# One layer-order change in a two-layer encoder: operands of a pair one step earlier, other orders at the first and last blocks, a third value tile

## The chip, the cores and the metric

The kernel runs on one core of one Trainium2 chip. The metric is the device time of one launch in microseconds (us); the kernel before took 4037.84 us in the median of three runs (4030.55 to 4040.72). The core has five engines with a queue each: TensorE (PE, matrix products into the PSUM banks), VectorE (DVE), ScalarE (ACT), GpSimd (POOL) and SyncE (SP), which here only issues transfers. Each engine works through its own list of instructions in order, and waits at an instruction until what it needs is there.

## The reference, cut to what matters

Two layers work on 256 prompt tokens and 1024 sample tokens, with 1024 channels, in float32. Layer 0 mixes tokens with a bidirectional RWKV recurrence, layer 1 with a two-dimensional neighbourhood attention; each is followed by the same kind of channel mixer, and that is where most of this change lies:

```python
def _sq_relu_mlp(h, w_up, w_down):
    return jnp.square(jax.nn.relu(h @ w_up)) @ w_down

for layer in range(DEPTH):
    h = _rms_norm(x, p['norm_mix_g'][layer])
    y = mixer(h)                    # RWKV in layer 0, attention in layer 1
    x = x + y
    x = x + _sq_relu_mlp(_rms_norm(x, p['norm_mlp_g'][layer]), p['w_up'][layer], p['w_down'][layer])
```

The hidden width is 4096. Both products of the mixer are 1280 tokens by 1024 by 4096.

## The kernel before, in words

A float32 product is made from three matmuls of rounded halves. Each operand is cut into a high half (a cast on ACT) and a low half (operand minus high half, on DVE or POOL); the products high·high, high·low and low·high are summed in PSUM. So every operand costs a cast and a subtraction before PE can use it. In the names, `ah`/`al` are the halves of the normed activations, `whi`/`wlo` those of `w_up` (L90, L91), `dh`/`dl` those of `w_down` or of sums of its tiles, and `hh`/`hl` those of the hidden values (L1371, L1372; True marks a sample half, False the prompt).

The tokens are worked in three segments: 0 is the prompt (256 columns), 1 and 2 are the halves of the sample (512 columns each). The hidden width is worked in 32 blocks `f` of 128. `up(f, s)` makes block `f` for segment `s`: 24 matmuls, a relu on ACT (L1387), a square on POOL (L1388), and, where it is wanted at once, the cut into halves. The cut of a prompt block is made within `up` in every case. `wup(f)` loads and cuts the next `w_up` tile, its low half on POOL. `wraw(f, i)` only issues the load of half `i` of a `w_down` tile on SP, from a ring of six buffers, and `wdown` loads and cuts. `down` (L1420 adds the product to the residual `x`) is the plain second product of one or two blocks for one segment; the last one also scales `x`, writes it out (L1423) and, in layer 0, prepares the attention's normed activations.

Blocks 2 to 29 are worked in pairs by a scheme with seven products in place of eight for the sample halves. `prep(n)` forms the two operands of product `n`, as sums (L1435) where needed, and cuts both: the weights' side in `wcut` (ACT, POOL) and the values' side in `bcut` (ACT, DVE). `product(n)` issues 12 matmuls (L1480 to L1482) into four banks of kind `pc`, and adds each to a part of `x` on DVE (L1484), four adds. A product that starts a new group of sums needs its four banks empty, so it waits for the adds of the product before it that used them. `prompt(n)` multiplies the same weights with the prompt's block (24 matmuls of 256 columns) and has two adds (L1495) on DVE.

`block_pair` gives the order by hand: while the products of one pair run, it interleaves the `up` steps of the next two blocks `f2` and `f3 = f2 + 1`. `prep(0)` of the next pair (`ahead[0](0)`) is the last operand made in this order, behind `prompt(7)`. In the last pair there is no next pair (`final`), and three `up` steps of blocks 30 and 31 are left. PE, DVE, ACT and POOL follow this written order closely; SP's order and all of the attention's orders are made by a scheduler that places work by its own estimates of times.

At a layer's end the last two blocks go through plain downs in the order of the segments. In layer 0 the norms of each segment's tokens (`N(s)`, with a small matmul at L1196) and the first quarter of the attention's values (`V(tb)`, one of ten blocks of 128 tokens: 24 matmuls at L513 to L515, a scaled copy `vt` on ACT at L519, a write at L520) follow inside them. The other three quarters of the values come afterwards, with `vt` in a ring of two.

Of the kernel before, what the change touches and what calls it, by code (L numbers as in the profile page):

```python
# [5 lines left out]
F32 = mybir.dt.float32  # L6
# [7 lines left out]
P = 128  # L14
# [37 lines left out]
class Trunk:  # L52
# [1222 lines left out]
    def channel_layer(self, layer, x_src, src, wname, dst, gnext=None, gate=False):  # L1275
# [3 lines left out]
        nc, tc, a, act = self.nc, self.tc, self.a, self.act  # L1279
        NF = 32  # L1280
        gmlp = V_GMLP + 8 * layer
        with ExitStack() as ctx:
# [42 lines left out]
            def wup(f):  # L1325
                wu[f] = self.wsplit(wp, a["w_up"][layer, f], 1024, nc.gpsimd, tag="u", rb=1)
# [28 lines left out]
            def scale(s):  # L1355
                c0, c1 = SEGS[s]
                n = c1 - c0
                ps = pn.tile([P, 512], F32, name="nps", tag="nps")
                nc.tensor.matmul(ps[:, :n], ones, ms[s], start=True, stop=True)
                nc.vector.tensor_scalar(out=ms[s], in0=ps[:, :n], scalar1=1.0 / (KT * P), scalar2=RMS_EPS, op0=ALU.mult, op1=ALU.add)  # L1360
                for m in range(8):
                    (nc.gpsimd if m % 2 else nc.vector).tensor_tensor(out=x[s][:, m], in0=x[s][:, m], in1=ms[s], op=ALU.mult)
# [5 lines left out]
            def split(src, s, pool, tags, bufs, eng):  # L1368
                n = src.shape[1]
                hi, lo = (pool.tile([P, n], F32R, name=t, tag=t, bufs=bufs) for t in tags)  # L1370
                nc.scalar.copy(hi, src)  # L1371
                eng.tensor_tensor(out=lo, in0=src, in1=hi.bitcast(F32), op=ALU.subtract)  # L1372
                return hi, lo

            def cut(f, s, last=False):
                r = hid[f, s]
                if last:
                    hid[f, s] = split(r, s, wh_, ("tt", "tt"), 2, nc.vector)
                else:
                    hid[f, s] = split(r, s, wh_, (f"hh{s > 0}", f"hl{s > 0}"), 3 if s else 4, nc.vector)  # L1380

            def up(f, s, name=None, whole=True):
                c0, c1 = SEGS[s]
                n = c1 - c0
                ps = dense(*wu[f], s, name)
                r = wk.tile([P, n], F32, name="rl", tag="nt", bufs=6) if s else wh_.tile([P, n], F32, name="rl", tag="np", bufs=2)
                nc.scalar.activation(r, ps[:, :n], AF.Relu)  # L1387
                nc.gpsimd.tensor_tensor(out=r, in0=r, in1=r, op=ALU.mult)  # L1388
                hid[f, s] = r
                if whole or s == 0:  # L1390
                    cut(f, s)
# [106 lines left out]
            def block_pair(f2, cur, ahead):  # L1498

                (prep, product, prompt), f3, final = cur, f2 + 1, ahead is None  # L1500
                U = lambda f, s: up(f, s, "ps", False)
                prep(1)
                product(0)
                U(f2, 1)
                wraw(f3, 0)
                prompt(0)
                prep(2)
                product(1)
                U(f2, 2)
                wraw(f2, 1)  # L1510
                prep(3)
                product(2)
                U(f2, 0)
                if not final:
                    wup(f2 + 2)
                prep(4)
                product(3)
                U(f3, 1)
                wraw(f3, 1)
                prompt(3)  # L1520
                prep(5)
                product(4)
                prep(7)
                if not final:
                    U(f3, 2)
                prep(6)
                product(5)
                U(f3, 0)
                wraw(f2, 0)
                if not final:  # L1530
                    wup(f3 + 2)
                prompt(7)
                if not final:
                    ahead[0](0)
                product(6)
                prompt(6)

# [3 lines left out]
            vw = []  # L1541
# [3 lines left out]
            N = lambda s: lambda: norms(s)  # L1545
            V = lambda tb: lambda: block(tb)
            up(0, 0)
            wup(1)
            scale(0)
            wdown(0)  # L1550
            up(1, 0)
            up(0, 1)
            up(1, 1)
            scale(1)
            up(0, 2)
# [8 lines left out]
            with tc.manual_schedule(engines=MANUAL):  # L1564
# [17 lines left out]
                for f in range(2, NF - 2, 2):  # L1582
                    ahead = pair_steps(f + 2, f + 3) if f < NF - 4 else None
# [4 lines left out]
            with tc.manual_schedule(engines={mybir.EngineType.PE}):  # L1588
                wdown(NF - 2, False)
                cut(NF - 2, 1)  # L1590
                wdown(NF - 1, False)
                cut(NF - 1, 1)
                cut(NF - 2, 2)
                up(NF - 1, 2, None, False)
                cut(NF - 1, 2, True)
                down([NF - 2, NF - 1], 0)
                if gnext is None:
                    down([NF - 2, NF - 1], 1)
                    down([NF - 2, NF - 1], 2)
                else:  # L1600

                    v0 = [self.wsplit(wp, a["w_nv"][0, :, 4 * j:4 * j + 4, :].rearrange("p k c -> p (k c)"), 1024, nc.gpsimd, tag="u", rb=1) for j in range(2)]
                    vw += [tuple(t[:, 256 * (k % 4):256 * (k % 4) + 256] for t in v0[k // 4]) for k in range(KT)]
                    down([NF - 2, NF - 1], 1, {6: [N(0)]})
                    down([NF - 2, NF - 1], 2, {1: [V(0)], 3: [V(1)], 4: [N(1)], 5: [V(2)]})
                    for f in (V(3), V(4), N(2), V(5), *map(V, range(6, 10))):
                        f()


# [24 lines left out]
    def attention(self):  # L1634
        nc, tc, a, act = self.nc, self.tc, self.a, self.act
        v1_d = self.scr["v1_d"]
        vs_d = self.dram("vs_d", [20, P, 1024])
        at_d = self.dram("at_d", [8, 2, P, T])
        with ExitStack() as ctx:
            pool = lambda name, c=ctx, bufs=1, **kw: c.enter_context(tc.tile_pool(name=name, bufs=bufs, reuse_waits="tile", **kw))  # L1640
            self.awp = pool("atw", bufs=2, side="right")
            self.apd = pool("apd", bufs=2, space=PSUM)
            self.gq = self.awp.tile([P, 1], F32, name="gq", bufs=1)
            nc.vector.tensor_scalar(out=self.gq, in0=self.vec[:, V_QG:V_QG + 1], scalar1=0.125, scalar2=None, op0=ALU.mult)
            self.awp.tile([P, 20], F32, name="rs", tag="rs", bufs=4)
            J, work, tail = self.qk_proj(0)

            self.qke = [pool("qk0"), None]
            self.qlo = [self.low_queries(self.qke[0]), None]
            bp = pool("abp")  # L1650

            self.bs = [bp.tile([P, 2, 3, 12, 32], F32, name=f"bs{r}") for r in range(2)]
            self.bpm = bp.tile([P, 2, 2, 128], F32, name="bpm")
            for t in self.bs:
                nc.vector.memset(t, NEG)
            with ExitStack() as c2:
                vp = pool("atv", c2)
                pv = pool("apv", c2, 3, space=PSUM)


                vp.tile([P, 256], F32, name="vt", tag="vt", bufs=2)
                vw = [None, self.v_weights(a["w_nv"], vp, 1)]
                work.pop(1)()
                bias = self.load_bias(0, 0, []) + self.load_bias(0, 1, []) + self.load_bias(0, 2, [])
                for q in range(1, 4):
                    if q < 3:
                        vw.append(self.v_weights(a["w_nv"], vp, q + 1))
                    for tb in range(10):
                        self.v_block(act, vw[q], v1_d, (vp, "vt", 256, 2), (pv, "vps"), q, tb, self.tn[:, 0, tb:tb + 1])
                        if tb == 3:  # L1670
                            self.strips(q - 1, nc.scalar)
                        for f in bias[:2]:
                            f()
                        del bias[:2]
            self.qk = self.qke[1] = pool("aqk", bufs=2)
            self.qlo[1] = self.low_queries(self.qk)
            self.awk = pool("awk", bufs=2)
            self.apn = pool("apn", space=PSUM)
            self.aps = pool("aps", bufs=2, space=PSUM)
            self.apt = pool("apt", bufs=2, space=PSUM)  # L1680
            self.apo = pool("apo", space=PSUM)
            self.attend_all(J, work, tail)
# [410 lines left out]
```

## Time and profile before

| what | us |
|---|---|
| median of three runs | 4037.84 (4030.55, 4037.84, 4040.72) |
| profiled execution, its time | 4028.49 |
| its span | 4026.7 |
| PE busy | 3754.7 |
| DVE busy | 2394.2 |
| ACT busy | 1686.2 |
| POOL busy | 1697.3 |
| mean granted clock of PE | 0.969 |

The mixer of layer 0 begins at about 1500 us and its blocks end at 2360; the attention's values and its other products follow up to about 3042; the mixer of layer 1 runs from about 3130 to the end. A row of a timeline gives start, duration, engine, line, operation, output and inputs, shape, count, and in brackets how long the engine stood idle before it and what ended that. A matmul's duration overlaps with the next one's; PE's pace is read from the distance of two starts. A row of a window gives the stretch, its length, the busy time and count of PE, PEld (weight loads), DVE, ACT and POOL, then the granted clock of PE (1.00 is full), the busy share of the transfer engines, and GB/s.

### The profile page before, as it was taken

The page shows a single profiled execution, that of the slowest core. Times are in us where ns is not written, and L with a number is a line of the kernel's source. Part 1 is how long each engine was busy: PE and PEld are TensorE (multiplying, and loading weights), DVE is VectorE, ACT ScalarE, POOL GpSimd, SP SyncE. Part 2 cuts the span into 40 slices and gives each one's busy share as a digit, 9 for nine tenths or more (in the row PEclk, how much of TensorE's full clock was granted, in tenths as well). Part 3 has the DMA queues.
Part 4 walks back from the last instruction along what each step waited for, and adds up shares of the span by engine and source line. Part 5 has one row for each costly group of instructions (what it writes and reads, how often), then busy time and mean ns, then how long its engine had stood idle before and what let it go on. Part 6 is the DMA issues. An engine that isn't in the chain of part 4 may idle for free.

```text
span 4026.7 us, 89828 instructions
## 1 busy us (share of the span) xinstructions
PE 3754.7 (93%) x36484; PEld 3158.2 (78%) x36484; DVE 2394.2 (59%) x4441; ACT 1686.2 (42%) x4128; POOL 1697.3 (42%) x1540
## 2 busy tenths in 40 slices
PE   8988888889888899999999988999989999999999
PEld 5764578778888787888888878887778788888887
DVE  5778743656464445666666671355553656666666
ACT  6777642555555431222222242466663222222221
POOL 4446641122222424545555561344442455555454
PEclk9988999999999899999999999999999999999999
DMA  4236565776664430111111115345465111111111
GB/s 138 73 98 226 211 222 136 163 172 159 160 148 122 130 104 27 42 37 40 38 37 42 40 61 159 114 108 112 98 157 169 37 40 37 43 40 43 37 40 61
DMA packets 460094, 394.83 MB, mean 98 GB/s; under 512 B 268480, under 2 KB 353856, under 8 KB 459680
## 3 DMA queue, kind: packets, MB, share of 16 engines
q1 hardware_dynamic: 425264, 327.73, 29.5%
q10 hardware_dynamic: 34416, 61.35, 4.2%
q8 instruction: 288, 4.72, 0.5%
q14 instruction: 126, 1.03, 0.1%
HBM read 270.50 MB, written 124.44 MB: 98 GB/s over the span
## 4 chain that ended last, share of the span: by engine, by line
PE 67%; DVE 8%; ACT 7%; issue 6%; DMA 5%; POOL 5%; SPq 1%; ACTq 0%; POOLq 0%; DVEq 0%
PE ps L96 12%; PE ps L97 11%; PE ps L98 11%; PE wu L998 4%; PE ps L1480 4%; PE ps L1482 3%; PE ps L1481 3%; POOL rl L1388 1%; PE vps L513 1%; ACT whi L90 1%; PE aps L998 1%; POOL dl L1372 1%; PE vps L514 1%; PE vps L515 1%; PE op L2005 1%
## 5 line engine op out<-in xcount | busy, mean ns | idle before, releaser
L96 PE MATMUL ps<-ah,whi 128*128 128x512 f32 (+1 forms) x2304 | 845.1, 367 | 4.7 <-ACT whi L90 3.9
L98 PE MATMUL ps<-ah,wlo 128*128 128x512 f32 (+1 forms) x2304 | 826.2, 359 | 9.5 <-POOL wlo L91 9.3
L97 PE MATMUL ps<-al,whi 128*128 128x512 f32 (+1 forms) x2304 | 827.6, 359 | 0.0
L98 PEld LDWEIGHTS ps<-ah,wlo 128*128 128x128 f32 x2304 | 435.3, 189 | 84.0 <-POOL wlo L91 10.5
L96 PEld LDWEIGHTS ps<-ah,whi 128*128 128x128 f32 x2304 | 436.6, 189 | 79.9 <-issue 9.0
L97 PEld LDWEIGHTS ps<-al,whi 128*128 128x128 f32 x2304 | 436.8, 190 | 65.7 <-issue 1.0
L1484 DVE TENSOR_TENSOR x<-ps,x 128x512 f32<-128x512 f32 x784 | 484.9, 678 | 0.0
L1388 POOL TENSOR_TENSOR rl<-rl 128x512 f32<-128x512 f32 (+1 forms) x192 | 173.8, 905 | 658.7 <-ACT rl L1387 381.6
L1387 ACT ACTIVATE rl<-ps 128x512 f32<-128x512 f32 (+1 forms) x192 | 101.0, 526 | 799.2 <-PE ps L98 799.2
L91 POOL TENSOR_TENSOR wlo<-raw,whi 128x1024 fp32r<-128x1024 f32 (+1 forms) x114 | 235.2, 2063 | 228.0 <-ACT whi L90 220.5
L1480 PE MATMUL ps<-hhTrue,dh 128*128 128x512 f32 x784 | 309.6, 395 | 21.8 <-DVE x L1484 21.8
L1482 PE MATMUL ps<-hhTrue,dl 128*128 128x512 f32 x784 | 308.0, 393 | 0.5 <-POOL dl L1372 0.5
L1481 PE MATMUL ps<-hlTrue,dh 128*128 128x512 f32 x784 | 308.0, 393 | 0.0
L1372 DVE TENSOR_TENSOR hlTrue<-rl,hhTrue 128x512 fp32r<-128x512 f32 x98 | 122.1, 1247 | 202.6 <-ACT hhTrue L1371 202.3
L1372 POOL TENSOR_TENSOR dl<-raw,dh 128x512 fp32r<-128x512 f32 x128 | 221.0, 1729 | 11.0 <-ACT dh L1371 7.0
L1372 DVE TENSOR_TENSOR hlTrue<-ts,hhTrue 128x512 fp32r<-128x512 f32 x112 | 131.2, 1171 | 150.3 <-ACT hhTrue L1371 150.3
L90 ACT CAST whi<-raw 128x1024 fp32r<-128x1024 f32 (+1 forms) x142 | 133.2, 938 | 190.0 <-PE ps L97 81.6
L1371 ACT CAST dh<-ds 128x512 fp32r<-128x512 f32 x112 | 69.5, 620 | 295.5 <-POOL ds L1435 295.5
L1480 PEld LDWEIGHTS ps<-hhTrue,dh 128*128 128x128 f32 x784 | 147.8, 188 | 53.9 <-issue 27.1
L1495 DVE TENSOR_TENSOR x<-ps,x 128x512 f32<-128x512 f32 x224 | 148.7, 685 | 68.0 <-PE ps L98 66.7
L1372 POOL TENSOR_TENSOR dl<-ds,dh 128x512 fp32r<-128x512 f32 x112 | 157.3, 1405 | 63.5 <-ACT dh L1371 63.5
L1942 POOL TENSOR_TENSOR s<-s,mx 128x384 f32<-128x384 f32 (+1 forms) x150 | 109.7, 744 | 163.0 <-DVE mx L1941 115.7
(339 smaller groups left out, 10268.1 us busy)
## 6 DMA issues: line engine op xcount, KB each, us to landing
raw<-in_w_down_dram SPq DMA_DIRECT2D x128, 256.0 KB, 2.7
raw<-in_w_up_dram SPq DMA_DIRECT2D x64, 512.0 KB, 3.4
ar<-ar_d SPq DMA_DIRECT2D x80, 256.0 KB, 4.2
bk<-bk_d SPq DMA_DIRECT2D x80, 256.0 KB, 3.6
ar_d<-ar ACTq DMA_DIRECT2D x32, 512.0 KB, 3.1
bk_d<-bk ACTq DMA_DIRECT2D x32, 512.0 KB, 4.7
bs<-tab SPq DMA_DIRECT2D x128, 96.0 KB, 3.8
v_d<-vt ACTq DMA_DIRECT2D x80, 128.0 KB, 3.3
```

The costliest lines, as they stand in the source:

```text
L90: nc.scalar.copy(hi[:, cs], raw)
L91: lo_eng.tensor_tensor(out=lo[:, cs], in0=raw, in1=hi[:, cs].bitcast(F32), op=ALU.subtract)
L96: mm(ps, sh, mh, start=first, stop=False)
L97: mm(ps, sh, ml, start=False, stop=False)
L98: mm(ps, sl, mh, start=False, stop=last)
L998: self.nc.tensor.matmul(out, w, x, start=start, stop=stop, skip_group_check=free)
L1372: eng.tensor_tensor(out=lo, in0=src, in1=hi.bitcast(F32), op=ALU.subtract)
L1388: nc.gpsimd.tensor_tensor(out=r, in0=r, in1=r, op=ALU.mult)
L1480: mm(ch[j], hi[:, cs], hh, start=bool(new), stop=False, skip_group_check=True)
L1481: mm(ch[j], hi[:, cs], hl, start=False, stop=False, skip_group_check=True)
L1482: mm(ch[j], lo[:, cs], hh, start=False, stop=True, skip_group_check=True)
L1484: nc.vector.tensor_tensor(out=xv, in0=ch[j], in1=xv, op=ALU.add)
```

## The change

There are four edits to the order of steps, and one buffer more.

- In `block_pair`, for all pairs but the last, `prep(0)` of the next pair moves from behind `prompt(7)` to ahead of `U(f3, 0)`, and `wraw(f2, 0)` is issued ahead of it too. PE's own order is the same in these pairs.
- In the last pair `U(f3, 0)` moves from behind `product(5)` to ahead of `prep(6)`.
- At the first blocks `up(0, 1)` moves up, from behind `up(1, 0)` to right behind `wup(1)`.
- At the last blocks the down of segment 0 moves ahead of `up(31, 2)`; in layer 0 the value blocks and norms are put in another order: `V(0)` stands ahead of the down of segment 2, `V(1)` inside it, and `N(1)` behind it.
- In the attention `vt` gets three buffers in place of two.

```diff
                 prep(7)
-                if not final:
-                    U(f3, 2)
+                U(f3, 0 if final else 2)
                 prep(6)
                 product(5)
-                U(f3, 0)
                 wraw(f2, 0)
                 if not final:
+                    ahead[0](0)
+                    U(f3, 0)
                     wup(f3 + 2)
                 prompt(7)
-                if not final:
-                    ahead[0](0)
                 product(6)
                 prompt(6)
...
             up(0, 0)
             wup(1)
+            up(0, 1)
             scale(0)
             wdown(0)
             up(1, 0)
-            up(0, 1)
             up(1, 1)
...
+                down([NF - 2, NF - 1], 0)
                 up(NF - 1, 2, None, False)
                 cut(NF - 1, 2, True)
-                down([NF - 2, NF - 1], 0)
...
                     down([NF - 2, NF - 1], 1, {6: [N(0)]})
-                    down([NF - 2, NF - 1], 2, {1: [V(0)], 3: [V(1)], 4: [N(1)], 5: [V(2)]})
-                    for f in (V(3), V(4), N(2), V(5), *map(V, range(6, 10))):
+                    V(0)()
+                    down([NF - 2, NF - 1], 2, {1: [V(1)]})
+                    for f in (N(1), *map(V, range(2, 6)), N(2), *map(V, range(6, 10))):
                         f()
...
-                vp.tile([P, 256], F32, name="vt", tag="vt", bufs=2)
+                vp.tile([P, 256], F32, name="vt", tag="vt", bufs=3)
```

How DVE's list changes at one passage from a pair to the next, in layer 0. Before (`hlTrue<-ts` is the low half for product(6), the first four L1484 adds are product(5)'s, the two L1495 adds prompt(7)'s, `hlTrue<-rl` is the first operand of the next pair, and the last adds are product(6)'s):

```order
L1372 TENSOR_TENSOR hlTrue<-ts,hhTrue 128x512
L1484 TENSOR_TENSOR x_22225<-ps,x_22225 128x512 x4
L1372 TENSOR_TENSOR hlFalse<-rl,hhFalse 128x256
L1495 TENSOR_TENSOR x_22223<-ps,x_22223 128x512 x2
L1372 TENSOR_TENSOR hlTrue<-rl,hhTrue 128x512
L1484 TENSOR_TENSOR x_22224<-ps,x_22224 128x512 x4
```

and now:

```order
L1372 TENSOR_TENSOR hlTrue<-ts,hhTrue 128x512
L1484 TENSOR_TENSOR x_22225<-ps,x_22225 128x512 x4
L1372 TENSOR_TENSOR hlTrue<-rl,hhTrue 128x512
L1372 TENSOR_TENSOR hlFalse<-rl,hhFalse 128x256
L1495 TENSOR_TENSOR x_22223<-ps,x_22223 128x512 x2
L1484 TENSOR_TENSOR x_22224<-ps,x_22224 128x512 x4
```

The next pair's cut has moved ahead of the prompt's cut and of prompt(7)'s adds, and product(6)'s adds now follow those directly.

POOL's list at the first blocks of layer 0. Before (the first `rl` is the square of up(0,0), L1362 is the scaling of `x` in scale(0), and `wlo` the low half of the tile of wup(1)):

```order
L1388 TENSOR_TENSOR rl<-rl 128x256
L1362 TENSOR_TENSOR x_22223<-x_22223,ms_22234 128x256 x2
L91 TENSOR_TENSOR wlo<-raw,whi 128x1024
L1362 TENSOR_TENSOR x_22223<-x_22223,ms_22234 128x256 x2
L1388 TENSOR_TENSOR rl<-rl 128x256
```

and now:

```order
L1388 TENSOR_TENSOR rl<-rl 128x256
L91 TENSOR_TENSOR wlo<-raw,whi 128x1024
L1388 TENSOR_TENSOR rl<-rl 128x512
L1362 TENSOR_TENSOR x_22223<-x_22223,ms_22234 128x256 x4
L1388 TENSOR_TENSOR rl<-rl 128x256
```

The low half of the tile stands directly behind the first square, with the square of up(0,1) and all four scalings behind it.

DVE's list in the last pair of layer 0, from the adds of prompt(3) on. Before (the L1484 adds are those of product(4), product(5) and, after L1495, product(6)):

```order
L1435 TENSOR_TENSOR ts<-rl 128x512
L1372 TENSOR_TENSOR hlTrue<-ts,hhTrue 128x512
L1484 TENSOR_TENSOR x_22225<-ps,x_22225 128x512 x4
L1435 TENSOR_TENSOR ts<-rl,ts 128x512
L1372 TENSOR_TENSOR hlTrue<-ts,hhTrue 128x512
L1484 TENSOR_TENSOR x_22225<-ps,x_22225 128x512 x4
L1372 TENSOR_TENSOR hlTrue<-rl,hhTrue 128x512
L1372 TENSOR_TENSOR hlFalse<-rl,hhFalse 128x256
L1495 TENSOR_TENSOR x_22223<-ps,x_22223 128x512 x2
```

and now:

```order
L1435 TENSOR_TENSOR ts<-rl 128x512
L1372 TENSOR_TENSOR hlTrue<-ts,hhTrue 128x512
L1484 TENSOR_TENSOR x_22225<-ps,x_22225 128x512 x4
L1372 TENSOR_TENSOR hlFalse<-rl,hhFalse 128x256
L1435 TENSOR_TENSOR ts<-rl,ts 128x512
L1372 TENSOR_TENSOR hlTrue<-ts,hhTrue 128x512
L1484 TENSOR_TENSOR x_22225<-ps,x_22225 128x512 x4
L1495 TENSOR_TENSOR x_22223<-ps,x_22223 128x512 x2
```

The prompt's cut stands between product(4)'s adds and the operand of product(6); the cuts of block 30 for the sample have moved behind product(6)'s adds.

More of the change, by code (lines that the diff above doesn't have):

```diff
@@ L1668, in attention @@
                     for tb in range(10):
-                        self.v_block(act, vw[q], v1_d, (vp, "vt", 256, 2), (pv, "vps"), q, tb, self.tn[:, 0, tb:tb + 1])
+                        self.v_block(act, vw[q], v1_d, (vp, "vt", 256, 3), (pv, "vps"), q, tb, self.tn[:, 0, tb:tb + 1])
                         if tb == 3:
```

## The prediction

> **What bounds the kernel now.** I read the page first, then the waits of TensorE over the whole span, then the rows around each wait.
>
> ```profile
> span 4026.7 us, 89828 instructions
> ...
> PE 3754.7 (93%) x36484; PEld 3158.2 (78%) x36484; DVE 2394.2 (59%) x4441; ACT 1686.2 (42%) x4128; POOL 1697.3 (42%) x1540
> ```
>
> TensorE (PE) is busy for 93% of the span, and its work is the same after the change. So a gain can only be PE idle time that goes away, and the half-rate stretches that follow a long idle. The list of PE's waits, columns "total, times, longest", begins with the lines that the change concerns:
>
> ```profile
> PE ps L1480 <- DVE x L1484: 21.8, 28, 2.2
> ...
> PE ps L98 <- POOL wlo L91: 9.3, 4, 3.7
> ```
>
> The first is the channel mixers' own. By windows that hold the blocks of the first and of the second mixer it splits so:
>
> ```profile
> PE ps L1480 <- DVE x L1484: 8.6, 13, 0.7
> ```
> ```profile
> PE ps L1480 <- DVE x L1484: 11.0, 14, 2.2
> ```
>
> Thirteen waits of 0.66 us in the first, thirteen of (11.0 − 2.2)/13 = 0.68 in the second: one at each passage from a pair of blocks to the next. The remaining 2.2 stands in the last block.
>
> **Part A, the passage between pairs.** The rows of one passage, PE first:
>
> ```profile
> 1816.41 0.28 PE L98 MATMUL ps<-hhFalse,dl 128*128 128x256 f32 x1
> 1817.35 0.47 PE L1480 MATMUL ps<-hhTrue,dh 128*128 128x512 f32 x1 [0.66 <-DVE x L1484]
> ```
>
> The matmuls before start 0.12 us apart, so product(0) could start at 1816.53 and starts 0.82 later (0.82 to 0.84 at the other passages; I use 0.83). It needs a bank that product(6)'s adds (L1484) empty. VectorE's (DVE's) rows tell why they are late:
>
> ```profile
> 1807.74 2.48 DVE L1484 TENSOR_TENSOR x<-ps,x 128x512 f32<-128x512 f32 x4
> 1812.66 0.43 DVE L1372 TENSOR_TENSOR hlFalse<-rl,hhFalse 128x256 fp32r<-128x256 f32 x1 [2.44 <-ACT hhFalse L1371]
> 1813.00 1.28 DVE L1495 TENSOR_TENSOR x<-ps,x 128x512 f32<-128x512 f32 x2
> 1814.65 1.96 DVE L1372 TENSOR_TENSOR hlTrue<-rl,hhTrue 128x512 fp32r<-128x512 f32 x1 [0.36 <-ACT hhTrue L1371]
> 1816.53 1.87 DVE L1484 TENSOR_TENSOR x<-ps,x 128x512 f32<-128x512 f32 x3
> ```
>
> The low half of the next pair's first operand (hlTrue) is queued ahead of product(6)'s adds. It waits for its high half, then runs 1.96 us. ScalarE (ACT) and GpSimd (POOL) in the same stretch:
>
> ```profile
> 1806.47 0.62 ACT L1371 CAST hhTrue<-ts 128x512 fp32r<-128x512 f32 x1
> 1811.11 0.38 ACT L1387 ACTIVATE rl<-ps 128x256 f32<-128x256 f32 x1 [4.02 <-PE ps L98]
> ...
> 1812.53 1.04 ACT L90 CAST whi<-raw 128x1024 fp32r<-128x1024 f32 x1
> 1813.48 0.62 ACT L1371 CAST dh<-raw 128x512 fp32r<-128x512 f32 x1
> 1814.00 0.61 ACT L1371 CAST hhTrue<-rl 128x512 fp32r<-128x512 f32 x1
> ```
> ```profile
> 1807.14 1.83 POOL L1372 TENSOR_TENSOR dl<-raw,dh 128x512 fp32r<-128x512 f32 x1
> 1811.58 0.61 POOL L1388 TENSOR_TENSOR rl<-rl 128x256 f32<-128x256 f32 x1 [2.60 <-ACT rl L1387]
> 1813.65 2.40 POOL L91 TENSOR_TENSOR wlo<-raw,whi 128x1024 fp32r<-128x1024 f32 x1 [1.47 <-ACT whi L90]
> ```
>
> The change puts the four operations ahead of the product for the prompt's columns. On ACT dh and hhTrue (0.62 + 0.61) then start at 1807.1 and end at 1808.3; the 4.02 idle ahead of 1811.11 covers them. POOL's dl (1.73 to 1.83) runs from 1808.97 to 1810.8, inside the 2.60 idle ahead of 1811.58. DVE's hlTrue follows the adds that end at 1810.22 and takes 1.0 to 2.0, inside the 2.44 idle ahead of 1812.66. So no covering engine becomes late: uncovered, the same operations would cost 1.2, 1.8 and 2.0 us. The two L1495 adds still end at 1814.28. Product(6)'s four adds follow at once, the first bank is free at about 1814.9 and the second at 1815.5, against 1816.53 and 1817.2 at which PE asks. The slack is 1.6 us, so the wait goes wholly. What is late next would be POOL's first difference of the new pair, and it becomes earlier, since dl no longer stands before it. The gain is 26 × 0.83 = **21.6**; bounds 11 (half of it stays) and 22.
>
> [...]
>
> The moved cast also needs its weights a step earlier. Their load is issued far ahead:
>
> ```profile
> 1744.64 10.59 SPq L1395 DMA_DIRECT2D raw<-in_w_down_dram  x3
> ```
> ```profile
> raw<-in_w_down_dram SPq DMA_DIRECT2D x128, 256.0 KB, 2.7
> ```
>
> It has landed some 50 us before 1807. On SP nothing but wraw(f2, 0) moves, to where its slot is equally free: 0.
>
> **Part B, the first blocks.** In the first mixer, PE, then POOL, then the clock behind the wait (a row of a window, with its mean granted clock 0.50):
>
> ```profile
> 1516.15 0.39 PE L98 MATMUL ps<-ah,wlo 128*128 128x256 f32 x1 [3.68 <-POOL wlo L91]
> ```
> ```profile
> 1511.81 1.81 POOL L1362 TENSOR_TENSOR x<-x,ms 128x256 f32<-128x256 f32 x2
> 1513.58 2.52 POOL L91 TENSOR_TENSOR wlo<-raw,whi 128x1024 fp32r<-128x1024 f32 x1
> ```
> ```profile
> 1516.60:1519.80 3.20, 3.20 (x17) 3.20 (x16) 0.65 (x1) 0.00 (x0) 1.24 (x2) 0.50 0.49 164
> ```
>
> PE loses 3.84 and 0.35 of pitch around the wait, and 1.46 in the slow stretch (22 matmuls in 4.10 where 2.64 is usual): 5.65. After it, up(0,1), about 5.6 us of dense matmuls on data that are ready, fills the time from 1509.3 on, and wlo stands before the two L1362 products, so it ends near 1514.4. PE asks for it near 1515.4. In the second mixer the same place is
>
> ```profile
> 3151.75 0.58 PE L98 MATMUL ps<-ah,wlo 128*128 128x256 f32 x1 [2.85 <-POOL wlo L91]
> ```
>
> 3.3 here, 1.2 at the matmul that waits for whi at 3147.70, and 1.4 of half rate: 5.9. Sum **11.5**. The first block's own wait for wlo (1.4 in each) stays. Bounds 6 (the half rate stays and a wait of 1.4 comes in each) and 12.
>
> **Part C, the last blocks and the start of the attention.** In the final pair the wait is larger:
>
> ```profile
> 2342.99 0.47 PE L1480 MATMUL ps<-hhTrue,dh 128*128 128x512 f32 x1 [2.20 <-DVE x L1484]
> ```
> ```profile
> 3976.20 0.47 PE L1480 MATMUL ps<-hhTrue,dh 128*128 128x512 f32 x1 [2.20 <-DVE x L1484]
> ```
>
> up(f3,0) moved there has 2.87 us of matmuls and covers it. But it no longer stands between product(5) and product(6), whose four adds take 2.48 in a row like the one quoted at 1807.74: new waits of 0.8 to 1.1 at product(6) and about 1.3 at the first plain product. I count 0.2 a layer, plus 1.3 of a half-rate stretch behind the second mixer's wait: **1.5** for the second mixer, bounds 0 and 5. That stretch followed 2.20 us of idling, and the first mixer's equal wait had none. [...]
>
> In the first mixer the tail runs on into the values of the attention. PE's waits from 2340 to 2482, and the window of the tail (columns PE, PEld, DVE, ACT, POOL busy, clock, DMA share, GB/s):
>
> ```profile
> PE vps L513 <- ACT vt L519: 7.5, 2, 6.0
> PE nps L1196 <- POOL acc L1168: 6.7, 2, 6.3
> PE ps L96 <- DVE x L1420: 6.2, 3, 5.5
> ```
> ```profile
> 2360.80:2421.60 60.80, 47.28 (x283) 40.85 (x281) 54.23 (x79) 30.96 (x64) 42.50 (x33) 0.91 0.29 99
> ```
>
> DVE has 54.23 of 60.80 us and sets the pace; PE has 13.5 of idling. The change lets DVE begin the down sums some 3.6 us earlier (no up(31,2) before them) and puts the value blocks where PE waited 5.5 and 6.3. So PE comes to the second quarter's values about 12 earlier. Whether that counts is set by what follows there:
>
> ```profile
> 2456.02 0.47 ACT L519 ACTIVATE vt<-vps,tn 128x256 f32<-128x256 f32 x1 [0.54 <-DMA v_d<-vt]
> 2456.82 0.47 ACT L519 ACTIVATE vt<-vps,tn 128x256 f32<-128x256 f32 x1 [0.33 <-DMA v_d<-vt]
> ...
> 2467.90 0.62 ACT L90 CAST whi<-raw 128x512 fp32r<-128x512 f32 x1 [10.60 <-DMA raw<-in_w_nq_dram]
> ...
> 2474.13 0.62 ACT L90 CAST whi<-raw 128x512 fp32r<-128x512 f32 x1 [5.61 <-DMA raw<-in_w_nq_dram]
> ```
> ```profile
> 2452.00:2462.00 10.00, 9.79 (x81) 9.79 (x82) 0.27 (x1) 2.09 (x5) 1.29 (x1) 1.00 0.81 200
> ```
>
> ACT holds the vt copies behind two casts that wait for loads, and the loads lie behind the writes of x and others. The third vt buffer removes at most 0.54 + 0.33 = 0.9. The load chain starts after the last write of x, which comes with DVE's chain, 4 to 6 earlier. So C lies between 4 (the loads move by as much as DVE's first add, nothing more) and 16 (12 plus the vt waits); I take **10**, midway. The attention's order comes from the scheduler and shifts a little too (some vh casts go ahead of two vt copies); I price that inside these bounds.
>
> **The sum.** 21.6 + 11.5 + 1.5 + 10 = 44.6. The profiled execution took 4028.5 us (the span and 1.8 around it), so it would come to 3984. The median of the runs shown is 4037.84, 9.3 above it: 3993 there. I say 3992.
>
> **The rivals.**
> 1. *The attention takes C back.* The loads of the nq weights are bound by transfers (share 0.81 in the row above), and PE arrives earlier only to wait longer at vt. For it: 16.2 us of ACT's waiting there is for these loads. Against it: SP queues them behind the writes, which come earlier. C is then 0 to 2: 4038 − 35 = **4003**. [...]
> 2. *The passage's wait only moves.* The adds of product(6) come in time, but the moved cuts make another product late, and half of A or all goes. Against it: the covers above, each over 0.4 us too long. Time **4004** to 4015.
> 3. *Slower: the casts at the head of ACT's queue wait for their load.* If the weights of the next pair landed after 1807.1, ACT would hold up the relu of up(f3,0) and product(0) its operands. Landing, cast 0.62, dl 1.8: the gain is gone from a landing at 1815.4, and the whole kernel is 12 us slower when each passage loses 2.2, at 1816.2. Time from **4050**. Against it: 2.7 us of landing from an issue at 1744.64.
> 4. *Nothing comes of it*: DVE falls behind elsewhere as PE gets denser, within 12 us of before. DVE's 59% speaks against it.
>
> **How the numbers follow.** A run here differs from another by about 0.3%, 12 us, so less counts as no change. Forecast 0.64 (3975 to 4000), rival 1 0.20, rival 2 0.10, rival 3 0.02, rival 4 0.04. Low end: A 22, B 12, C 16 + 5, and runs at the low side give 3975; the high end takes in rival 1 and the near half of rival 2: 4010. Faster 0.64 + 0.20 + 0.10 = 0.94, same 0.04, slower 0.02.
>
> **What would show it.** Right: no wait of L1480 at the passages and a period shorter by 0.83; product(6)'s adds starting where the L1495 adds end; no half rate near 1516 and 3152; no 5.5 and 6.3 waits in the tail. The prediction is wrong if a passage still has over 0.3 of waiting, if up(1,0) still waits for wlo by over 1 us, or if the vt wait in the second quarter grows beyond 15.

## The result, and the profile after

The changed kernel took 3986.52 us in the median of five runs (3975.61 to 3993.14); the kernel before, run beside it, 4035.45 (4030.55 to 4040.72). The ratio is 0.9872, 95% interval 0.9851 to 0.9893: faster by 1.3%, some 49 to 52 us. The forecast was 3992 us, within 3975 to 4010. The profiled span fell from 4026.7 to 3976.5, by 50.2 us.

The head of the page after:

```profile
span 3976.5 us, 89848 instructions
...
PE 3742.6 (94%) x36484; PEld 3151.9 (79%) x36484; DVE 2371.8 (60%) x4441; ACT 1686.8 (42%) x4128; POOL 1686.1 (42%) x1540
```

Busy time of DVE fell by 22 us with the same instructions. One group alone, the cuts that the change moves, fell by 33 us: 26 of its 98 became shorter. Others rose, the sums `ts<-rl` (L1435) most, by 7.7. The group before, then after (the columns behind the bar are busy time and mean ns, then idle time before them):

```profile
L1372 DVE TENSOR_TENSOR hlTrue<-rl,hhTrue 128x512 fp32r<-128x512 f32 x98 | 122.1, 1247 | 202.6 <-ACT hhTrue L1371 202.3
```
```profile
L1372 DVE TENSOR_TENSOR hlTrue<-rl,hhTrue 128x512 fp32r<-128x512 f32 x98 | 88.8, 909 | 185.0 <-ACT hhTrue L1371 184.7
```

PE's waits in the blocks of the first mixer, the window that held thirteen waits of 0.66 us before:

```profile
PE ps L98 <- POOL wlo L91: 1.4, 1, 1.4
PE ps L96 <- DVE x L1420: 1.1, 2, 0.9
PE ps L1480 <- DVE x L1484: 0.9, 1, 0.9
PE ps L1482 <- POOL dl L1372: 0.2, 1, 0.2
```

The one L1480 wait left is that of the last pair. The passage of which the rows were shown before, now: PE, DVE, POOL.

```profile
1806.79 0.28 PE L98 MATMUL ps<-hhFalse,dl 128*128 128x256 f32 x1
1806.91 0.40 PE L1480 MATMUL ps<-hhTrue,dh 128*128 128x512 f32 x1
1807.14 0.40 PE L1481 MATMUL ps<-hlTrue,dh 128*128 128x512 f32 x1
```
```profile
1798.12 2.48 DVE L1484 TENSOR_TENSOR x<-ps,x 128x512 f32<-128x512 f32 x4
1800.51 0.69 DVE L1372 TENSOR_TENSOR hlTrue<-rl,hhTrue 128x512 fp32r<-128x512 f32 x1
1803.04 0.42 DVE L1372 TENSOR_TENSOR hlFalse<-rl,hhFalse 128x256 fp32r<-128x256 f32 x1 [1.84 <-ACT hhFalse L1371]
1803.38 1.28 DVE L1495 TENSOR_TENSOR x<-ps,x 128x512 f32<-128x512 f32 x2
1804.58 2.48 DVE L1484 TENSOR_TENSOR x<-ps,x 128x512 f32<-128x512 f32 x4
```
```profile
1797.53 3.09 POOL L1372 TENSOR_TENSOR dl<-raw,dh 128x512 fp32r<-128x512 f32 x2
1801.95 0.61 POOL L1388 TENSOR_TENSOR rl<-rl 128x256 f32<-128x256 f32 x1 [1.34 <-ACT rl L1387]
1804.04 2.41 POOL L91 TENSOR_TENSOR wlo<-raw,whi 128x1024 fp32r<-128x1024 f32 x1 [1.47 <-ACT whi L90]
```

PE passes from one pair to the next at its steady 0.12 us. The cut of hlTrue takes 0.69 us in place of 1.96: it now stands in a gap of POOL, between the two dl (done at 1800.62) and the square. Product(6)'s adds follow the L1495 adds at once.

At the first blocks, the window that holds the place of the 3.68 us wait, and POOL's row of the tile's low half:

```profile
1506.50:1521.00 14.50, 14.50 (x84) 12.68 (x83) 11.41 (x13) 4.99 (x9) 10.58 (x9) 1.00 0.23 73
```
```profile
1510.89 2.40 POOL L91 TENSOR_TENSOR wlo<-raw,whi 128x1024 fp32r<-128x1024 f32 x1
```

PE is busy for all of the 14.50 us at the full clock, and wlo is ready at 1513.3. At the layer's end and the start of the attention (PE's waits from 2330 to 2490):

```profile
PE vps L513 <- ACT vt L519: 4.4, 1, 4.4
PE vps L513 <- DVE x L1420: 4.0, 2, 2.7
PE nps L1196 <- POOL acc L1168: 2.2, 1, 2.2
PE ps L1480 <- DVE x L1484: 0.9, 1, 0.9
PE ps L96 <- ACT vt L519: 0.6, 1, 0.6
```

The 5.5 for DVE's sums is gone, the 6.3 for the norm is 2.2, the two waits for vt (7.5) are one of 4.4, and two new ones for DVE's sums come to 4.0. On ACT the copies of vt still stand behind the two casts of nq weights, and PE's wait of 4.4 ends behind them, at 2444.32:

```profile
2437.33 0.62 ACT L90 CAST whi<-raw 128x512 fp32r<-128x512 f32 x1 [5.78 <-DMA raw<-in_w_nq_dram]
2443.10 0.62 ACT L90 CAST whi<-raw 128x512 fp32r<-128x512 f32 x1 [5.16 <-DMA raw<-in_w_nq_dram]
2443.79 0.84 ACT L519 ACTIVATE vt<-vps,tn 128x256 f32<-128x256 f32 x2
```

**Where the 50.2 us come from.** Every kernel here issues the same 36484 matmuls, in lists that differ only within short stretches. So the time at which PE starts its n-th matmul can be compared between any two profiles, at places outside those stretches. The gain over the profile of the kernel before, in us, by stretch:

| stretch (time in the kernel before) | change | change, profiled again | only the passages (first experiment) |
|---|---|---|---|
| up to the first mixer's blocks (1500) | 0.96 | 1.85 | −4.45 |
| first blocks, first mixer | 5.82 | 5.96 | −0.02 |
| 13 passages, first mixer | 12.14 | 12.08 | 12.10 |
| last pair to third quarter of the values (2336 to 2506) | 11.55 | 13.74 | −3.55 |
| rest of the attention, to the second mixer's blocks | −0.77 | −2.24 | −0.71 |
| first blocks, second mixer | 5.87 | 5.88 | −0.12 |
| 13 passages, second mixer | 12.00 | 11.96 | 11.94 |
| last pair to the end, second mixer | 2.63 | 2.63 | 0.02 |
| sum | 50.2 | 51.9 | 15.2 |

The stretches inside the mixers repeat to 0.2 us; the first stretch and the start of the attention do not. A measured time mixes the two; the table keeps them apart, and the experiments are read by it.

How far the stretch from the last pair to the third quarter of the values scatters, four kernels of the next section show, in which its order is that of the change: the values' cut early alone, the weights' cut early alone, both behind product(6), and the scalings first. It gained 12.98, 9.45, 12.63 and 10.24 there. So the change is worth 9.5 to 13.7 in this stretch over six profiles, and another kernel has to leave that range before it says something. Part of the scatter is half rate: of this stretch 23.9 us ran at half rate in the kernel before, and 10.2 to 23.9 in the six.

### The profile page after: what moved, and what is told of

The parts are those of the page before. It is cut to its first block, busy times and chain, and to the rows that moved or that the text cites. A ratio compares the mean times of both kernels' runs of the same rounds, so it can differ in the third digit from the quotient of the medians.

```text
span 3976.5 us, 89848 instructions
## 1 busy us (share of the span) xinstructions
PE 3742.6 (94%) x36484; PEld 3151.9 (79%) x36484; DVE 2371.8 (60%) x4441; ACT 1686.8 (42%) x4128; POOL 1686.1 (42%) x1540
## 4 chain that ended last, share of the span: by engine, by line
PE 73%; DVE 8%; DMA 7%; ACT 5%; issue 4%; POOL 2%; SPq 1%; ACTq 0%; DVEq 0%; POOLq 0%
PE ps L96 13%; PE ps L97 13%; PE ps L98 12%; PE ps L1480 4%; PE ps L1481 4%; PE ps L1482 4%; PE wu L998 4%; PE vps L513 1%; PE aps L998 1%; PE vps L514 1%; PE vps L515 1%; PE kps L998 1%; DVE q L875 1%; PE op L2004 1%; DMA raw<-in_w_no_dram 1%
## 5 line engine op out<-in xcount | busy, mean ns | idle before, releaser
L1484 DVE TENSOR_TENSOR x<-ps,x 128x512 f32<-128x512 f32 x784 | 484.9, 679 | 0.0
L1480 PE MATMUL ps<-hhTrue,dh 128*128 128x512 f32 x784 | 307.4, 392 | 1.8 <-DVE x L1484 1.8
L1481 PE MATMUL ps<-hlTrue,dh 128*128 128x512 f32 x784 | 307.3, 392 | 0.0
L1482 PE MATMUL ps<-hhTrue,dl 128*128 128x512 f32 x784 | 306.8, 391 | 0.5 <-POOL dl L1372 0.5
L1372 POOL TENSOR_TENSOR dl<-raw,dh 128x512 fp32r<-128x512 f32 x128 | 208.7, 1643 | 9.4 <-ACT dh L1371 8.4
L1495 DVE TENSOR_TENSOR x<-ps,x 128x512 f32<-128x512 f32 x224 | 148.8, 686 | 95.1 <-PE ps L98 93.8
L1372 DVE TENSOR_TENSOR hlTrue<-rl,hhTrue 128x512 fp32r<-128x512 f32 x98 | 88.8, 909 | 185.0 <-ACT hhTrue L1371 184.7
L1482 PEld LDWEIGHTS ps<-hhTrue,dl 128*128 128x128 f32 x784 | 147.2, 188 | 33.7 <-POOL dl L1372 1.4
```

The costliest lines, as they stand in the source:

```text
L1480: mm(ch[j], hi[:, cs], hh, start=bool(new), stop=False, skip_group_check=True)
L1481: mm(ch[j], hi[:, cs], hl, start=False, stop=False, skip_group_check=True)
L1482: mm(ch[j], lo[:, cs], hh, start=False, stop=True, skip_group_check=True)
L1484: nc.vector.tensor_tensor(out=xv, in0=ch[j], in1=xv, op=ALU.add)
L1495: nc.vector.tensor_tensor(out=xv, in0=ps, in1=xv, op=ALU.add)
```

## The experiments

**The passages alone.** On the kernel before:

```diff
                 product(5)
-                U(f3, 0)
+                if final:
+                    U(f3, 0)
                 wraw(f2, 0)
                 if not final:
+                    ahead[0](0)
+                    U(f3, 0)
                     wup(f3 + 2)
                 prompt(7)
-                if not final:
-                    ahead[0](0)
```

> The kernel before with the move of prep(0) ahead of U(f3, 0) in all pairs but the last, and nothing else of the change. My theory: the gain at the passages is independent of the rest, 26 times 0.92 us (the period of a pair before less that after), so the span falls from 4026.7 to about 4003 and the other waits stay as they were. Rival: part of the 24 us depends on the first blocks or the tail (PE denser there); then the span is above 4008.

Measured: ratio 0.9941 (0.9920 to 0.9961), span 4011.5. By the table's last column the passages gain 24.0 us, as in the whole change, and the first blocks and the mixers' ends nothing. So the gain does not depend on the rest, though the span lies above 4008, which was to speak for the rival: −4.45 comes from before 1500 us, where nothing is changed, and −3.55 from the attention's start. There two more stretches of 3.41 us ran at half rate than in the profile of before, one of them in the last pair:

```profile
2335.35 0.47 PE L1480 MATMUL ps<-hhTrue,dh 128*128 128x512 f32 x1 [2.19 <-DVE x L1484]
```
```profile
2336.40:2339.60 3.20, 3.20 (x9) 2.51 (x8) 2.51 (x4) 0.62 (x1) 2.34 (x2) 0.50 0.00 0
```

The granted clock is 0.50 behind a wait that had no such stretch in this place before (1.00 from 2343.20 to 2346.40).

**Half of the moved operand, and the other way.** Three kernels take the change and place the two cuts of prep(0) differently: the values' cut early and the weights' cut behind prompt(7); the reverse; and both behind product(6). (In the first two the lines are four further on: L1484 there is the product's matmul L1480, L1486 is L1482, L1488 the adds L1484.)

```diff
...
                 if not final:
-                    ahead[0](0)
+                    ahead[0]('v')     # hhTrue, hlTrue alone; 'w' (dh, dl) in the second kernel
                     U(f3, 0)
                     wup(f3 + 2)
                 prompt(7)
+                if not final:
+                    ahead[0]('w')     # 'v' in the second kernel
                 product(6)
```

> The changed kernel, but in prep(0) only the values' cut (hhTrue, hlTrue) is made early; the weights' cut (dh, dl) stands behind prompt(7) as before. My theory: product(6)'s adds are then in time, but dl runs on POOL behind wlo and is ready near 1817.8 on the clock of the kernel before, while PE wants it near 1817.0; the wait moves to L1482 (on POOL dl), 0.75 us a passage, and almost all of the gain is lost: span about 3996. Rival: only the place of hlTrue in DVE's queue mattered; then the span stays at 3976 to 3979 with no wait at the passage.

> The changed kernel, but in prep(0) only the weights' cut is made early; the values' cut stands behind prompt(7) as before. If hlTrue's end is set by wlo on POOL (it ended 0.56 us after wlo in the kernel before), starting it 0.4 earlier changes nothing: product(6)'s adds come as late as before, the wait on L1484 stays at 0.6 to 0.7 us and the span is 3998 to 4001. If the two engines do not hold each other up, hlTrue ends 0.4 or more earlier, the wait falls to 0.3 or less and the span is 3976 to 3990.

> The changed kernel with prep(0) moved the other way, behind product(6), so that DVE does the adds first. My theory: the adds are in time, but the operands are not: hlTrue starts after them near 1816.8 on the clock of the kernel before and dl ends near 1817.75; PE waits 0.7 to 1.0 us a passage at L1481 or L1482 in place of L1480, span 3996 to 4003. Rival: the place of the cut ahead of the adds was the whole of it; then the span is at most 3982.

| gain at the 13 passages, us | first mixer | second mixer | a passage |
|---|---|---|---|
| both early (the change) | 12.14 | 12.00 | 0.93 |
| values' cut early only | 5.60 | 5.47 | 0.43 |
| weights' cut early only | 0.46 | 0.05 | 0.02 |
| both behind product(6) | −4.67 | −4.64 | −0.36 |

With the values' cut early alone, PE waits for dl, as my theory had it, but 0.22 us and not 0.75:

```profile
1816.32 0.50 PE L1486 MATMUL ps<-hhTrue,dl 128*128 128x512 f32 x1 [0.22 <-POOL dl L1372]
```
```profile
1812.60 2.42 POOL L91 TENSOR_TENSOR wlo<-raw,whi 128x1024 fp32r<-128x1024 f32 x1 [1.47 <-ACT whi L90]
1814.96 1.31 POOL L1372 TENSOR_TENSOR dl<-raw,dh 128x512 fp32r<-128x512 f32 x1
```

PE's starts are 0.61 and 0.34 us apart around this wait, where 0.23 is usual, so it costs 0.49, of the 0.50 that a passage loses against the change. (The span, 3994.0, is near the 3996 that I expected by luck: 6.2 us of it were lost before 1500 us.) That dl takes 1.31 us; in the kernel before it took 1.73, with hlTrue beside it at its start:

```profile
1816.02 1.73 POOL L1372 TENSOR_TENSOR dl<-raw,dh 128x512 fp32r<-128x512 f32 x1
```

With the weights' cut early alone nothing is gained, and the rows show why (DVE, then POOL):

```profile
1808.03 2.40 DVE L1372 TENSOR_TENSOR hlTrue<-rl,hhTrue 128x512 fp32r<-128x512 f32 x1
1810.36 2.47 DVE L1488 TENSOR_TENSOR x<-ps,x 128x512 f32<-128x512 f32 x4
```
```profile
1807.49 2.40 POOL L91 TENSOR_TENSOR wlo<-raw,whi 128x1024 fp32r<-128x1024 f32 x1 [1.47 <-ACT whi L90]
```

hlTrue could start as soon as the L1495 adds were done, without an idle time, and then took 2.40 us in place of 1.96: it ended 0.54 us after wlo (1809.89), as it had ended 0.56 after it in the kernel before. In both kernels it is so 26 times out of 26: hlTrue started 0.99 us after wlo in the kernel before and 0.54 after it here, and ended 0.55 after it in both. So its end was set by wlo and not by its start. In the changed kernel, in POOL's gap, the same cut took 0.69.

Behind product(6) the adds are in time and the cut is not:

```profile
1814.44 0.39 PE L1480 MATMUL ps<-hhTrue,dh 128*128 128x512 f32 x1
1815.82 0.50 PE L1481 MATMUL ps<-hlTrue,dh 128*128 128x512 f32 x1 [0.99 <-DVE hlTrue L1372]
```
```profile
1812.11 2.47 DVE L1484 TENSOR_TENSOR x<-ps,x 128x512 f32<-128x512 f32 x4
1814.51 1.26 DVE L1372 TENSOR_TENSOR hlTrue<-rl,hhTrue 128x512 fp32r<-128x512 f32 x1
```

A wait of 0.99 at L1481 replaces 0.66 at L1480, and the passage is 0.36 slower than before; I had expected a draw. So the place in DVE's queue alone is not the cause: the operand has to be cut earlier, not only the adds let past. Timed, the three gave ratios of 0.9888 (0.9869 to 0.9907), 0.9919 (0.9892 to 0.9947) and 0.9941 (0.9923 to 0.9958).

**The first blocks: PE's cover or POOL's order.** The change, with scale(0) and wdown(0) back ahead of up(0, 1) (this kernel and those of the next two headings were executed once each, so they are read by their stretches alone):

```diff
             wup(1)
-            up(0, 1)
             scale(0)
             wdown(0)
+            up(0, 1)
             up(1, 0)
```

> The changed kernel with scale(0) and wdown(0) back ahead of up(0, 1) at the first blocks; on POOL wlo of the second tile then stands behind two of the L1362 scalings again, and PE still has up(0, 1) before up(1, 0). If the cover on PE is the main thing, wlo ends near 1516.1 on the clock of the kernel before, PE asks at 1515.5, and 0.6 us of waiting with no half rate comes back in each mixer: the first blocks gain 5.2 of 5.85. If POOL's order is the main thing, over 2.5 us of the 5.85 are lost in each.

The first blocks gain 5.15 and 5.06 in place of 5.82 and 5.87. One small wait is back, and the clock stays whole:

```profile
1518.50 0.38 PE L98 MATMUL ps<-ah,wlo 128*128 128x256 f32 x1 [0.49 <-POOL wlo L91]
```

So up(0, 1) as cover for PE is worth 5.1 us even with POOL's old order, and the low half of the tile ahead of the scalings adds 0.7, as expected. POOL's new order without the cover was not run.

**The end of layer 0.** Three kernels, each the change with one piece undone: the old order of the value blocks and norms; up(31, 2) back ahead of the down of segment 0; two vt buffers.

```diff
-                    V(0)()
-                    down([NF - 2, NF - 1], 2, {1: [V(1)]})
-                    for f in (N(1), *map(V, range(2, 6)), N(2), *map(V, range(6, 10))):
+                    down([NF - 2, NF - 1], 2, {1: [V(0)], 3: [V(1)], 4: [N(1)], 5: [V(2)]})
+                    for f in (V(3), V(4), N(2), V(5), *map(V, range(6, 10))):
```

> The changed kernel with the old places of the value blocks and norms at the end of layer 0 (V(0), V(1), N(1), V(2) inside the down of segment 2, N(2) ahead of V(5)); the down of segment 0 stays ahead of up(31, 2). My theory: the waits of 5.5 us for DVE's sums and 6.3 us for the norm come back; of the 10.8 us that the stretch from the last pair to the third quarter of the values gained, 2 to 4 remain. Rival: the loads at the start of the attention set the time; then 8 or more remain.

```diff
-                down([NF - 2, NF - 1], 0)
                 up(NF - 1, 2, None, False)
                 cut(NF - 1, 2, True)
+                down([NF - 2, NF - 1], 0)
```

> The changed kernel with up(31, 2) back ahead of the down of segment 0 in both layers. My theory: DVE's chain starts 3.6 us later in layer 0 and 2 to 4 us of the gain there are lost; in layer 1, where PE sets the end, it makes under 0.5. Rival: the loads at the attention's start set the time, and layer 0 loses under 1.

```diff
-                vp.tile([P, 256], F32, name="vt", tag="vt", bufs=3)
+                vp.tile([P, 256], F32, name="vt", tag="vt", bufs=2)
...
```

> The changed kernel with two vt buffers in the attention as before. My theory: the buffer is worth at most 0.9 us (the two waits of ACT for a write in the second quarter), because the copies of vt are held by the casts ahead of them on ACT; the stretch from the last pair to the third quarter then still gains 10 or more of its 11.5. Rival: with PE arriving earlier the writes are in the way, and over 2 us are lost.

In the stretch from the last pair to the third quarter of the values these gain 5.87, 9.41 and 14.49, where the change's order gained 9.5 to 13.7. The old order of values and norms costs 3.6 to 7.9: more remains than my 2 to 4 and less than the rival's 8. The waits come back smaller than they were, and DVE's chain of sums starts 3.9 us earlier than in the kernel before, counted from the last pair:

```profile
PE vps L513 <- ACT vt L519: 6.2, 3, 4.6
PE vps L513 <- DVE x L1420: 4.2, 1, 4.2
PE nps L1196 <- POOL acc L1168: 3.8, 1, 3.8
PE ps L96 <- DVE x L1420: 1.4, 1, 1.4
```

The old place of up(31, 2) gives a gain at the low edge of that range, so a cost in layer 0 is not shown, neither my 2 to 4 nor the rival's under 1; in layer 1 it gains 0.30 (2.93 in place of 2.63). The third vt buffer shows no gain: with two, this stretch was better than in any of the six, with a wait for vt of 1.3 in place of the 4.4 and 3.6 of the two profiles of the change. Its order in the attention differs too, since the scheduler makes it anew, so the buffer by itself stays unmeasured; in this one profile nothing was lost without it.

**The last pair.** The change, with U(f3, 0) back behind product(5):

```diff
-                U(f3, 0 if final else 2)
+                if not final:
+                    U(f3, 2)
                 prep(6)
                 product(5)
+                if final:
+                    U(f3, 0)
```

> The changed kernel with U(f3, 0) back between product(5) and prompt(7) in the last pair of both layers. My theory: the wait of 2.2 us at product(5) comes back and the 0.9 us at product(6) goes; layer 1, whose end is the kernel's end, loses 1.3 if no half rate follows and up to 3 if one does, so its 2.63 fall to between 0 and 1.3. Rival: the 2.63 come from the order of the down and up(31, 2); then they stay at 2 or more.

The end of layer 1 gains 1.60 in place of 2.63, above the 0 to 1.3 that I gave my theory and below the rival's 2. The wait of 2.19 us is back, and this time no half rate follows it, where before one did (the place in this kernel, its clock, and the clock behind the same wait in the kernel before):

```profile
3941.89 0.47 PE L1480 MATMUL ps<-hhTrue,dh 128*128 128x512 f32 x1 [2.19 <-DVE x L1484]
```
```profile
3942.00:3945.40 3.40, 3.40 (x18) 2.88 (x19) 2.71 (x5) 1.34 (x4) 3.29 (x3) 1.00 0.00 0
```
```profile
3977.60:3980.80 3.20, 3.20 (x10) 2.53 (x10) 2.51 (x5) 1.21 (x3) 1.99 (x2) 0.50 0.00 0
```

So the 2.63 are three things: about 1.3 of wait (2.35 us of lost pitch become 1.04), about 1.6 of half rate that the one profile had and another need not have, and −0.3 from the down ahead of up(31, 2), which costs that only beside the new last pair: the 1.60 here are the half rate alone.

**A further step: the nq load.** If ACT holds the copies of vt behind two casts that wait for nq weights, moving that load helps. On the change:

```diff
-                work.pop(1)()
+                nqload = work.pop(1)
...
                             self.strips(q - 1, nc.scalar)
+                        if (q, tb) == (2, 5):
+                            nqload()
```

> The changed kernel with the load and the cut of the first nq weights moved from ahead of the second quarter of the values to the sixth block of the third quarter. My theory: ACT no longer holds the copies of vt behind two casts that wait for these loads; PE's wait of 4.4 us at L513 goes, with the half rate behind it (1.5 to 3), and q comes in time for its first use 100 us later: 5 to 7 us less, span about 3970. Rival: the vraw loads and the writes are in the way as well, the wait only becomes shorter, and 0 to 3 us are gained; or the loads come too late for the first query product, and it is slower.

The stretch gains 18.97, which is 5.2 to 9.5 more than with the change's order, and the wait for vt is gone from the list:

```profile
PE vps L513 <- DVE x L1420: 4.0, 2, 2.7
PE nps L1196 <- POOL acc L1168: 2.3, 1, 2.3
PE ps L1480 <- DVE x L1484: 0.9, 1, 0.9
PE ps L96 <- ACT vt L519: 0.6, 1, 0.6
PE ps L98 <- POOL wlo L91: 0.4, 1, 0.4
```

The median was 3977.98 us (3971.64 to 3982.38), ratio 0.9863 (0.9843 to 0.9883), which by itself does not set it apart from the change (0.9872). The profiled span, 3980.6, where I expected about 3970, hides the gain: 10.9 us were lost before 1500 us, in code that is the same.

On top of it, the matmuls of V(6) ahead of N(2), with the copy behind it, and up(31, 2) back ahead of the down in layer 1 alone; beside it the change unaltered:

```diff
...
+                    def norm_behind():
+                        evac = self.v_block(..., 0, 6, self.tn[:, 0, 6:7], later=True)
+                        norms(2)
+                        evac()
-                    for f in (N(1), *map(V, range(2, 6)), N(2), *map(V, range(6, 10))):
+                    for f in (N(1), *map(V, range(2, 6)), norm_behind, *map(V, range(7, 10))):
...
```

> The kernel with the nq load later, and two more edits: the matmuls of V(6) stand ahead of N(2), with its copy behind the norm, and in layer 1 alone up(31, 2) is back ahead of the down of segment 0. Theory: PE's wait of 2.2 us at N(2) is covered by V(6)'s 2.8 us, and layer 1 gains 0.3; the stretch up to the third quarter of the values gains 20 to 22 in place of 19.0 against the kernel before, and the time is 0.2% below that of the changed kernel (about 3976 against 3986). Rival: the norm comes 2.8 us later and the values behind it wait for it: no gain over the kernel with the nq load later alone.

> The changed kernel unaltered, once more, beside the one with the later nq load and norm on the same chip. Expected: 3975 to 3993 us; aligned matmul by matmul, the passages, the first blocks and the last stretch of layer 1 gain what they gained in the first profile to within 0.2 us, the stretch before 1500 us differs by several us though its code is the same, and the stretch at the attention's start differs by up to 3.4 us with the phase of the half-rate stretches.

The wait at N(2) is gone, but another came, and the stretch gains 16.42, against 18.97 of the kernel with the nq load alone; the difference is within the scatter. I had expected 20 to 22. The list now has

```profile
PE vps L513 <- DVE x L1420: 4.0, 2, 2.7
PE vps L513 <- ACT vh L496: 3.4, 1, 3.4
PE vps L515 <- DVE al L1176: 0.9, 1, 0.9
```

The 0.3 in layer 1 is there (2.91). Median 3977.87 us (3968.46 to 3983.26), ratio 0.9849 (0.9828 to 0.9869); the change beside it 3987.59 (3976.74 to 3990.20), ratio 0.9874 (0.9854 to 0.9894). The intervals overlap, so by the times alone this version is not shown to be the faster. By the aligned profiles both kernels with the later nq load gain more in the stretch that it concerns than any of the six without it, by 2.7 to 9.5 us, and N(2) moved later shows no further gain.

## Why the prediction was right

*The sum.* Predicted 21.6 + 11.5 + 1.5 + 10 = 44.6. Measured in the profile 24.1 + 11.7 + 2.6 + 11.6 = 50.0; the two stretches without an edit come to 0.2 together. The terms were all too small, A by 2.5, B by 0.2, the last pair by 1.1 and C by 1.6, and none of them made up for another.

*Part A.* The mechanism was right: the wait goes wholly, 26 times. The term was mis-sized by 0.10 a passage. I counted the late start of product(0)'s first matmul (0.83), and not that the second starts 0.31 after it where 0.23 is usual (1817.35 and 1817.66, against 1806.91 and 1807.14 now). That is 0.08 more, 0.91 in all against 0.93 measured. A step of the explanation was incomplete: I gave the cut's place in the queue and its high half's lateness as the causes. The run with only the weights' cut early shows that the end of wlo on POOL set the end of the cut, so that starting it 0.4 us earlier, still beside wlo, was worth nothing. Of the cover, I gave hlTrue 1.0 to 2.0 us in its new place; it took 0.69.

*Part B.* Right in size (5.8 and 5.9 against 5.65 and 5.9) and in cause, by the run with the scalings first: PE's cover brings nearly all of it. The first block's own wait of 1.4 stayed, as said.

*Part C.* The 10, taken midway between 4 and 16, met 11.6, and 9.5 to 13.7 over six profiles. The direction was reasoned; that the middle fitted is in part luck, since the half rate in this stretch (23.9 us before, 13.7 in the profile of the change) was not in the term. That ACT's casts for nq hold vt was right: with their load later, the wait is gone. The share for the third buffer, at most 0.9, was not found. The new waits at product(6) (0.89) came as expected, but the one that I put at the first plain product (1.3) did not: PE's list shows none there. With the half rate, which I took at 1.3 and which was about 1.6, this makes 2.6 in place of 1.5.

*The rivals.* The attention did not take C back: its loads moved with the writes of x. The last write of x in front of the attention's loads was issued by 2391.3 in place of 2418.4, and the first nq load at 2433.18 in place of 2460.93: 27 to 28 us earlier, of which 18.9 had been gained before this stretch. The passage's wait did not move on, and DVE did not fall behind. At the passage shown, the casts at the head of ACT's queue ran without a wait for their load; in that rival's own terms the landing at which the kernel is 12 us slower is about 1816.75 and not 1816.2. The sentence on the clock held in the runs too: behind the same wait of 2.19 to 2.20 us the granted clock was 0.50 in the run with the passages alone and 1.00 in the run with the old last pair. What told these apart is in the last section.

## What to carry to other kernels

When two engines cut operands side by side, look at where the slower cut ends and not only at what it waits for: an instruction that ends a fixed time after its neighbour's, whatever its start, is probably held by the neighbour (here it ended 0.55 us after it in two kernels, having started 0.99 and 0.54 us after it). Moving it into the neighbour's gap brought its end forward and made it shorter too (1.96 to 0.69 us). A wait cost more than its idle time, since the matmul behind it started late too (0.66 us of idling cost 0.93); take the cost from the period of the loop. And where parts of a program differ by ten microseconds from one execution to the next, compare profiles by the n-th matmul, read each edit in its own stretch, and learn from profiles with the same order how far that stretch scatters.

## What the runs showed of the hardware that was not expected

The stretch before 1500 us, with the same instruction lists in all kernels, came out between 2.8 us faster and 13.3 slower than in the profile of the kernel before, over thirteen profiles; most of the scatter between the profiles is there. The cause stays open. It is not the chip alone: on one and the same chip, four kernels came out between 2.8 us faster and 12.4 slower.

Half rate does not follow from the length of a wait alone. The same wait of 2.2 us in the last pair was followed by 3.41 us at half rate in three places (layer 1 before, and both layers with the passages alone) and by none in three others (layer 0 before, and both layers with the old last pair). In the profiles of the kernel before and of the change the stretches at half rate near the edits were 3.41, 6.83 or 10.24 us long.

The clock records of the traces tell the two apart. In the profiles of the kernel before and of the change every change of the granted clock stands on one grid of 3.413 us, to 0.01 us, with its first line 0.98 us after the program's start in the one and 2.64 in the other. The three waits followed by half rate had 2.11, 2.19 and 2.19 us of their idling in one step of the grid; a line of the grid divided the other three, with 1.73, 1.47 and 1.51 in the larger part. Behind 1500 us, in those two profiles, half rate followed each of the 17 steps at full clock in which PE idled for 2.11 us or more. Of some 140 with less idling, 1.85 us at most, it followed two: 1.01 us at 2980.8 in the kernel before and 1.57 at 2395.4 in the changed one, both outside the mixers' blocks. So, by these records, the 1.6 us of half rate that the last pair lost in layer 1 hung on where the grid happened to lie.
